# Split-precision hybrid layer and adaLN block: three attention rows in flight in layer two, value accumulators in two banks

## Chip, core and metric

One core of a Trainium2 chip runs the whole program, in one launch. The metric is the device time of one execution in microseconds (us); the lower the better. The kernel before takes 1076.02 us (median of 3 executions, 1075.15 to 1076.85).

## What is computed

All data are fp32: 512 tokens of width 1024. Layer one puts 16 meta tokens ahead of them and mixes a causal pooling branch with forgetting attention. Layer two is an adaLN block: eight stick-breaking heads and eight chunked heads with a relative-position bias, an output projection and a feed-forward part. Its heart:

```python
h = rmsnorm_2(x, g_norm1) * (1 + sc1) + sh1            # sc1, sh1, gt1, ... = silu(c) @ w_ada + b_ada
q_sb, k_sb, v_sb, q_ca, k_ca, v_ca = split(h @ w_in)   # 6 x 512 columns
# stick-breaking head, for each block of 128 queries
z = q_sb @ k_sb.T / 8
log_beta, log_1m = log_sigmoid(z), where(s < t, log_sigmoid(-z), 0)
w = where(s < t, exp(log_beta + suffix_sum(log_1m)), 0);  o_sb = w @ v_sb
# chunked head
q_ca, k_ca = rmsnorm_2(q_ca, g_q), rmsnorm_2(k_ca, g_k)
o_ca = softmax(q_ca @ k_ca.T / 8 + bias, masked to 9 chunks of 64) @ v_ca
x = x + gt1 * (concat(o_sb, o_ca) @ w_o)
h = rmsnorm_2(x, g_norm2) * (1 + sc2) + sh2
x = x + gt2 * (relu(h @ w1) ** 2 @ w2)
```

## The kernel before, in words

**Products.** A dense fp32 product is made of three matmuls (`mm3`, lines 149 to 152): every operand is split into a high part (a cast to fp32r, L131) and a low part (the rest, L128), and high x high, high x low and low x high are summed in one PSUM bank. Weights come through the staging buffers `wr` (four of them, 4 KB a partition), are cast by ACT (L131) and their low part is made by POOL or DVE (L128). A "dense triple" below is one such group of three.

**Order on PE.** Two generators run side by side in `weave`: `attn2()` issues the attention of layer two, `dense2()` the dense work around it. They share a planned clock, `clk[0]`, in nanoseconds of PE work. A generator that yields `at(t)` gets its turn again when the planned clock has reached t; till then the other one issues. The constants `LAT_*` (lines 37 to 44) are these allowances: how much planned PE time lies between a step and the step that needs its result. They order instructions only; the real waits are semaphores. What the other engines do, and in which order, is set by a scheduler out of the dependences and the program order, not by hand.

**Attention of layer two.** A unit is one row of scores: head pair p, head e of the pair, query block i (0 to 3, with 128(i+1) keys). 64 units, pairs in the order 0, 1, 4, 2, 5, 3, 6, 7; pairs 0 to 3 are stick-breaking (`stick`), 4 to 7 chunked (`soft`). A unit's scores are two matmuls (L438, L439) into a bank. For `stick`, ACT makes Abs, Exp, Ln (L947 to L949), DVE a maximum, a scan and a subtraction, ACT a last Exp (L953); for `soft`, DVE adds the bias and finds the maximum (L960), ACT makes the Exp (L962), DVE divides (L963, L964). The result x lies in a buffer of the tag "T" (five of 128x512). `turn` transposes x block by block on PE (L972), and ACT or DVE copies it into the head's tile `PT` (L975, L977). Two units later at the earliest (`LAG = 2`), and after the allowance `LAT_SB` or `LAT_CM`, a unit is turned. After the eight units of a pair, `pv2` multiplies them with the values (L908) and ACT copies the result (L911).

**Dense work beside it.** `DENSE` is the order of the pieces: q and k of the later pairs (`qk2_sb`, `qk2_ca`; 24 matmuls of 128x512 for one 128-column tile), and the values of columns 512 to 1023 in two pieces, `v2_chunk(2)` and `v2_chunk(3)`. The chunked heads' q and k are normed in `norm()`: ACT squares the tile, ACT and DVE split the squares (L131, L128, into `PTm`, two buffers), and PE sums them over each head with two matmuls (L870, L871), at `LAT_SQ` after the tile. `ada_step` puts the adaLN products in between (DVE L215, L217; PE L234). Then `wo_first` begins the output projection: its eight k take the normed attention results, and the weights of k = 4 to 7 are kept for the second half of the tokens in the tags "Y", "Y" (high and low of k = 4, 5), "Y" and "PT" (k = 6, 7).

**Value pieces.** `v2_chunk` (lines 801 to 813) makes 256 columns of values for four blocks of 128 tokens t. Weights come in two halves (kk = 0, 1); for each half, t runs over 0 to 3 with four dense triples of 128x256 each. Each t has a bank of its own. After the second half of a t, ACT copies its 256 columns out (L813).

**Opening.** x[0] is loaded, then the gain `norm_g`; four matmuls spread the gain over the partitions (L360), x[0] is squared by ACT (L323), normed (L329), transposed (L333), and the value products of layer one begin (L150 to L152).

Of the kernel before, what the change touches and what calls it, by code (L numbers as in the profile page):

```python
# [51 lines left out]
def hybrid_then_adaln_block(ctx, tc, a, out, tap=None):  # L52
    nc = tc.nc
# [80 lines left out]
    def weights(aps, shape, hi=None, lo=None, eng=None):  # L134
        raw = wts.tile([128] + shape, F32, name="wr", tag="wr", bufs=4)
# [13 lines left out]
    def mm3(ps, lh, ll, rh, rl, start, stop):  # L149
        pe.matmul(ps, lh, rh, start=start, stop=False)  # L150
        pe.matmul(ps, lh, rl, start=False, stop=False)  # L151
        pe.matmul(ps, ll, rh, start=False, stop=stop)  # L152
# [448 lines left out]
    def dense1():  # L601
# [199 lines left out]
    def v2_chunk(c):  # L801
        pss = [bank() for _ in range(4)]
        base = (1024, 1280, 2560, 2816)[c]
        for kk in range(2):
            wh, wl = weights([wcols(w_in2, 3 * D, base, 256, 4, 512 * kk)], [4, 256])
            for t in range(4):
                for q in range(4):
                    k = 4 * kk + q
# [173 lines left out]
    def attn2():  # L982
# [213 lines left out]
```

## Time and profile before

| | us |
|---|---|
| median of 3 executions | 1076.02 (1075.15 to 1076.85) |
| the profiled execution, its own time | 1077.35 |
| its span, first to last instruction | 1075.6 |
| PE busy | 1025.8 (95% of the span) |
| DVE busy | 538.7 (50%) |
| ACT busy | 532.5 (50%) |
| POOL busy | 306.4 (28%) |
| mean granted TensorE clock | 0.983 |

The shares are means over stages with different limits. In the trace the stages lie so: opening to 28 us, layer one to 400, the norms between the layers to 450, attention of layer two with its dense work from 450 to 690, the rest of the output projection and the feed-forward part to the end. A bracket at the end of a timeline row, as [1.93 <-DVE T L964], says how long the engine had been idle before it and which instruction's end released it.

### The profile page before, as it was taken

The numbers are of one execution on the slowest core, as the hardware profiler recorded it, in microseconds if no ns is written. First come the engines' busy times: TensorE is split into PE (matmuls) and PEld (weight loads), VectorE is DVE, ScalarE is ACT, GpSimd is POOL, SyncE is SP. The second block draws the span as 40 slices with busy tenths as digits, with TensorE's granted clock in tenths as the row PEclk, the third lists the DMA queues.
The fourth block names the chain that finished last, engine by engine and source line by source line (L and its number), as shares of the span: only waits on it lengthen the run. The fifth ranks groups of instructions, "written<-read, shape, count | busy, mean of one in ns | idle before, by whom it ended". The sixth has DMA issues, their size and how long they took to land.

```text
span 1075.6 us, 14076 instructions
## 1 busy us (share of the span) xinstructions
PE 1025.8 (95%) x5351; PEld 840.9 (78%) x5351; DVE 538.7 (50%) x1031; ACT 532.5 (50%) x1006; POOL 306.4 (28%) x146
## 2 busy tenths in 40 slices
PE   7999999999999998988799978999999999999998
PEld 6977987778888887977577756799888888888886
DVE  5365866873534588487867676672121002121115
ACT  6355654554454565476678776354334333222221
POOL 4222123423322541002112143112332233322330
PEclk9999999999999999999989989999999999999999
DMA  8332542454633656135332234433445322332212
GB/s 240 81 117 59 149 117 80 137 141 127 163 98 115 228 166 197 57 99 157 100 88 67 79 108 128 141 111 99 125 124 142 98 92 105 98 98 98 95 62 79
DMA packets 133973, 125.45 MB, mean 117 GB/s; under 512 B 6053, under 2 KB 110337, under 8 KB 133906
## 3 DMA queue, kind: packets, MB, share of 16 engines
q1 hardware_dynamic: 133906, 124.56, 38.7%
q8 instruction: 42, 0.69, 0.3%
q14 instruction: 25, 0.20, 0.1%
HBM read 119.82 MB, written 4.73 MB: 116 GB/s over the span
## 4 chain that ended last, share of the span: by engine, by line
PE 77%; DVE 11%; ACT 5%; DMA 3%; issue 2%; POOL 1%; SPq 0%; DVEq 0%; POOLq 0%; ACTq 0%
PE ps L150 23%; PE ps L151 22%; PE ps L152 22%; DMA wr<-in_w_in_dram 2%; DVE ada L217 2%; PE ps L972 2%; PE ps L908 2%; PE ps L519 1%; PE ps L438 1%; PE ps L439 1%; DMA wr<-in_w_ada_dram 1%; DVE T L951 1%; PE ps L234 1%; ACT wh L131 1%; DVE wl L128 1%
## 5 line engine op out<-in xcount | busy, mean ns | idle before, releaser
L128 POOL TENSOR_TENSOR wl<-wr,wh 128x1024 fp32r<-128x1024 f32 x105 | 258.1, 2460 | 672.6 <-ACT wh L131 666.3
L131 ACT CAST wh<-wr 128x1024 fp32r<-128x1024 f32 x142 | 148.6, 1048 | 304.4 <-PE ps L151 143.8
L150 PE MATMUL ps<-hh,wh 128*128 128x512 f32 (+1 forms) x352 | 130.1, 370 | 0.7 <-DVE nmx L483 0.7
L151 PE MATMUL ps<-hl,wh 128*128 128x512 f32 (+1 forms) x352 | 125.6, 357 | 0.0
L152 PE MATMUL ps<-hh,wl 128*128 128x512 f32 (+1 forms) x352 | 125.2, 356 | 0.0
L152 PE MATMUL ps<-wh,T 128*128 128x512 f32 x256 | 101.1, 395 | 0.0
L151 PE MATMUL ps<-wl,T 128*128 128x512 f32 x256 | 100.9, 394 | 0.0
L150 PE MATMUL ps<-wh,T 128*128 128x512 f32 x256 | 100.7, 393 | 0.0
L150 PE MATMUL ps<-QK,wh 128*128 128x512 f32 (+1 forms) x264 | 99.3, 376 | 0.0
L151 PE MATMUL ps<-PT,wh 128*128 128x512 f32 (+1 forms) x264 | 98.6, 373 | 0.0
L152 PE MATMUL ps<-QK,wl 128*128 128x512 f32 (+1 forms) x264 | 98.3, 373 | 0.0
L217 DVE SCALAR_TENSOR_TENSOR ada<-wr,vc,ada 128x512 f32<-128x512 f32 x84 | 78.0, 929 | 39.5 <-DMA wr<-in_w_ada_dram 38.6
L128 DVE TENSOR_TENSOR wl<-wr,wh 128x1024 fp32r<-128x1024 f32 x37 | 45.1, 1220 | 86.3 <-ACT wh L131 86.3
L150 PEld LDWEIGHTS ps<-hh,wh 128*128 128x128 f32 x352 | 66.6, 189 | 20.5 <-issue 10.8
L152 PEld LDWEIGHTS ps<-hh,wl 128*128 128x128 f32 x352 | 66.7, 189 | 9.8
L151 PEld LDWEIGHTS ps<-hl,wh 128*128 128x128 f32 x352 | 66.6, 189 | 7.8
L152 PEld LDWEIGHTS ps<-QK,wl 128*128 128x128 f32 x264 | 49.6, 188 | 9.8
L150 PEld LDWEIGHTS ps<-QK,wh 128*128 128x128 f32 x264 | 49.6, 188 | 9.7 <-ACT T L668 0.2
L151 PEld LDWEIGHTS ps<-wl,T 128*128 128x128 f32 x256 | 48.1, 188 | 11.5
L150 PEld LDWEIGHTS ps<-wh,T 128*128 128x128 f32 x256 | 48.2, 188 | 11.2
L152 PEld LDWEIGHTS ps<-wh,T 128*128 128x128 f32 x256 | 48.1, 188 | 11.3
L151 PEld LDWEIGHTS ps<-PT,wh 128*128 128x128 f32 x264 | 49.7, 188 | 9.1
(326 smaller groups left out, 2234.0 us busy)
## 6 DMA issues: line engine op xcount, KB each, us to landing
wr<-in_w_in_dram SPq DMA_DIRECT2D x64, 512.0 KB, 5.2
wr<-in_w_dram SPq DMA_DIRECT2D x64, 512.0 KB, 4.0
wr<-in_w_ada_dram SPq DMA_DIRECT2D x48, 512.0 KB, 3.8
wr<-in_w_out_dram SPq DMA_DIRECT2D x12, 512.0 KB
wr<-in_w_o_dram SPq DMA_DIRECT2D x12, 512.0 KB, 3.4
xr<-in_x_dram SPq DMA_DIRECT2D x8, 512.0 KB, 4.2
wr<-in_w_up_pool_dram SPq DMA_DIRECT2D x8, 256.0 KB, 2.6
wr<-in_w_up_attn_dram SPq DMA_DIRECT2D x8, 256.0 KB
```

The source lines that it names most:

```text
L128: (eng or pool).tensor_tensor(dst, raw, f(hi), op=OP.subtract)
L131: act.copy(dst_hi, raw)
L150: pe.matmul(ps, lh, rh, start=start, stop=False)
L151: pe.matmul(ps, lh, rl, start=False, stop=False)
L152: pe.matmul(ps, ll, rh, start=False, stop=stop)
L217: dve.scalar_tensor_tensor(acc, raw[:, q, :], cs, acc, op0=OP.mult, op1=OP.add)
L234: pe.matmul(ps[:, j:j + 1], acc[:, 128 * j:128 * j + 128], ones_f[:, :1], start=True, stop=True)
L438: pe.matmul(ps, A[e][:, sa], B[e][:, sb], start=True, stop=False)
L439: pe.matmul(ps, A[e][:, sa], L[e][:, sb], start=False, stop=stop)
L519: pe.matmul(po[64 * e:64 * e + 64, c0:], lhs, rhs, start=j < 0, stop=j == 3)
L908: pe.matmul(po[64 * e:64 * e + 64, 128 * j:], V2[j][:, hc], W[e][:, j, 128 * j:], start=j == 0, stop=j == 3)
L972: pe.transpose(pt[:, j, :], x[:, 128 * j:128 * j + 128], ident)
```

## The change

1. `attn2`: a unit is turned three units later at the earliest (`LAG` 3), and its allowance depends on the query block: `LAT_SB` (4000, 5500, 6500, 7500) and `LAT_CM` (3200, 3800, 4400, 5000) in place of 5200 and 3200. `LAT_CA`, `LAT_QK`, `LAT_SQ` and `LAT_PV` grow; `LAT_QK` and `LAT_PV` hold for layer one too.
2. A head's four rows x lie in one [128, 4, 512] tile of the tag "Y", which has four buffers and also holds `MX[1]` and the kept weights of the output projection; the buffers of "T" become 8, of "PTm" 4, of `wr` 5.
3. `v2_chunk` puts its four accumulators of 256 columns into two banks. Only the first matmul into a bank (k = 0 of an even t) carries the start flag.
4. The scratch space of the dynamic DMA descriptors is set to 1024 bytes a partition, which leaves room for 2.
5. Opening: `norm_g` is loaded ahead of x[0]; 6, 4 and 6 matmuls of a constant with itself (128x128 fp32) go to a bank that nobody reads: at the start, after the gain's matmuls, and after the first norm's transposes.

```diff
-LAT_CA = 5600.0
+LAT_CA = 6000.0
-LAT_SB = 5200.0
-LAT_CM = 3200.0
-LAT_QK = 2600.0
-LAT_SQ = 3800.0
+LAT_SB = (4000.0, 5500.0, 6500.0, 7500.0)
+LAT_CM = (3200.0, 3800.0, 4400.0, 5000.0)
+LAT_QK = 3800.0
+LAT_SQ = 5000.0
-LAT_PV = 600.0
+LAT_PV = 1500.0
...
-        raw = wts.tile([128] + shape, F32, name="wr", tag="wr", bufs=4)
+        raw = wts.tile([128] + shape, F32, name="wr", tag="wr", bufs=5)
...
-    BUFS = {"QK": 2, "PT": 3, "Y": 4, "V": 1, "T": 5, "Z": 2, "PTm": 2, "strip": 1, "Cm": 1, "Vm": 1}
+    BUFS = {"QK": 2, "PT": 3, "Y": 4, "V": 1, "T": 8, "Z": 2, "PTm": 4, "strip": 1, "Cm": 1, "Vm": 1}
...
+    sp.dma_start(gn, rows(a["norm_g"], 0, 1, D, 0, D))
     sp.dma_start(xr[0], rows(a["x"], 0, 128, D, 0, D))
-    sp.dma_start(gn, rows(a["norm_g"], 0, 1, D, 0, D))
+    idle = bank()
+    def warm(n):
+        for _ in range(n):
+            pe.matmul(idle[:, :128], ones_f, ones_f, start=True, stop=True)
+    warm(6)
...
         pe.matmul(gnb[b], ones_f[:1], gn[:, 512 * b:512 * b + 512], start=True, stop=True)
+    warm(4)
...
     first_norm(xr[0], 128, NM, *x0)
+    warm(6)
...
     def v2_chunk(c):
-        pss = [bank() for _ in range(4)]
+        pss = [b[:, 256 * q:256 * q + 256] for b in (bank(), bank()) for q in range(2)]
...
-                    mm3(pss[t][:, :256], h, l, wh[:, q, :], wl[:, q, :], k == 0, k == KT - 1)
+                    mm3(pss[t], h, l, wh[:, q, :], wl[:, q, :], k == 0 and t % 2 == 0, k == KT - 1,
+                        skip_group_check=True)
...
-                st[p, e] = wt([128, 4, 512], "PT")
+                st[p, e] = wt([128, 4, 512], "PT"), wt([128, 4, 512], "Y")
...
-            x = P[p, i, e] = wt([128, 512], "T")
+            x = st[p, e][1][:, i, :]
...
-        LAG = 2
+        LAG = 3
...
-                ripe[n] = clk[0] + (LAT_SB if p < 4 else LAT_CM)
+                ripe[n] = clk[0] + (LAT_SB if p < 4 else LAT_CM)[units[n][1]]
...
-    nc = bacc.Bacc("TRN2", target_bir_lowering=False, num_devices=1)
+    nc = bacc.Bacc("TRN2", target_bir_lowering=False, num_devices=1, dynamic_dma_scratch_size=1024)
```

Lines of the change stand 10 or 11 further on than those of the kernel before: L438 becomes L448, L972 becomes L982, L908 becomes L919, L813 becomes L824, L975 becomes L985.

Three places in the order of the instructions follow.

**PE, first head of pair 4.** From the scores of its fourth unit (L438, 128x512) to that unit's four transposes (L972 x4), before:

```order
L438 MATMUL ps<-QK 128x512
L439 MATMUL ps<-lz_590,QK 128x512
L972 MATMUL ps<-ident,T 128x128 x2
L438 MATMUL ps<-QK 128x256
L439 MATMUL ps<-lz_591,QK 128x256
L972 MATMUL ps<-ident,T 128x128 x3
L438 MATMUL ps<-QK 128x256
L439 MATMUL ps<-lz_591,QK 128x256
L150 MATMUL ps<-h2h,wh 128x512
L151 MATMUL ps<-h2l,wh 128x512
L152 MATMUL ps<-h2h,wl 128x512
L972 MATMUL ps<-ident,T 128x128 x4
```

and with the change, first the rows from those scores on (after them come the eight value products L919 of a pair),

```order
L448 MATMUL ps<-QK 128x512
L449 MATMUL ps<-lz_607,QK 128x512
L150 MATMUL ps<-h2h,wh 128x512
L151 MATMUL ps<-h2l,wh 128x512
L152 MATMUL ps<-h2h,wl 128x512
L150 MATMUL ps<-h2h,wh 128x512
L151 MATMUL ps<-h2l,wh 128x512
L152 MATMUL ps<-h2h,wl 128x512
L982 MATMUL ps<-ident,Y 128x128
```

and then the rows from behind the value products to the four transposes:

```order
L448 MATMUL ps<-QK 128x256
L449 MATMUL ps<-lz_608,QK 128x256
L234 MATMUL ps<-ones_f,ada 128x1 x4
L982 MATMUL ps<-ident,Y 128x128 x2
L448 MATMUL ps<-QK 128x256
L449 MATMUL ps<-lz_608,QK 128x256
L982 MATMUL ps<-ident,Y 128x128 x3
L448 MATMUL ps<-QK 128x384
L449 MATMUL ps<-lz_608,QK 128x384
L982 MATMUL ps<-ident,Y 128x128 x4
```

A further dense triple, the eight value products and the scores of a third unit now stand between a unit's scores and its transposes.

**PE, the first value piece, from t = 0 to t = 1 of the second half.** Before, each t has its own bank (ps_4504, ps_4505):

```order
L150 MATMUL ps_4504<-wh_4620,h2h_3374 128x256
L151 MATMUL ps_4504<-wl_4621,h2h_3374 128x256
L152 MATMUL ps_4504<-wh_4620,h2l_3376 128x256
L972 MATMUL ps_4636<-ident_78,T_4542 128x128 [waits Activation_49]
L150 MATMUL ps_4505<-wh_4620,h2h_3374 128x256
L151 MATMUL ps_4505<-wl_4621,h2h_3374 128x256
L152 MATMUL ps_4505<-wh_4620,h2l_3376 128x256
```

With the change t = 0 and t = 1 lie in ps_4515, and the first matmul of t = 1 waits for ACT:

```order
L150 MATMUL ps_4515<-wh_4638,h2h_3391 128x256
L151 MATMUL ps_4515<-wl_4639,h2h_3391 128x256
L152 MATMUL ps_4515<-wh_4638,h2l_3393 128x256
L150 MATMUL ps_4515<-wh_4638,h2h_3391 128x256 [waits Activation_49]
L151 MATMUL ps_4515<-wl_4639,h2h_3391 128x256
L152 MATMUL ps_4515<-wh_4638,h2l_3393 128x256
```

What it waits for is the copy of t = 0 (L824, V2<-ps_4515). This wait stands four times in the program, from t = 0 to 1 and from t = 2 to 3 in each of the two pieces.

**ACT, the end of the attention.** The casts of the kept weights of k = 6, 7 (L131, Y<-wr). Before, among the softmax rows of the last pair:

```order
L131 CAST mxs_6163<-Y_6101 128x512 [waits DMAHW6_49]
L131 CAST Y_6456<-wr_6458 128x1024 [waits DMAHW6_49]
L962 ACTIVATE T_6249,sums_6251<-T_6249,nmx_6250 128x128 [waits DVE_49]
L131 CAST Y_6456<-wr_6492 128x1024 [waits DMAHW7_49]
L962 ACTIVATE T_6264,sums_6266<-T_6264,nmx_6265 128x256 [waits DVE_49]
```

With the change, behind the copy of the last transposes of the attention (Y_6427 takes the buffer that these read):

```order
L985 COPY PT_6318<-ps_6394 128x2x128 [waits PE_49]
L131 CAST wh_6659<-wr_6657 128x1024 [waits DMAHW0_49]
L985 COPY PT_6318<-ps_6421 128x4x128 [waits PE_49]
L131 CAST Y_6427<-wr_6429 128x1024 [waits DMAHW4_49,DVE_49]
L131 CAST Y_6427<-wr_6457 128x1024 [waits DMAHW1_49]
```

The low part of the first (POOL, L128 PT<-wr,Y) follows it, and the matmuls of k = 6 stand on PE directly behind those transposes. In the same way the low part of k = 4, 5 takes the buffer of the head before, so that POOL waits for that head's last transposes (L982); on PE two score matmuls of 512 columns and one matmul of k = 4 stand between these and its use.

## Rows read from the trace of the kernel before

**Rows 1.** Stages: us; busy of PE, PEld, DVE, ACT, POOL (count); clock; DMA share; GB/s.

```profile
28.00:400.00 372.00, 367.16 (x1983) 300.22 (x1982) 221.83 (x427) 192.09 (x365) 121.11 (x54) 1.00 0.44 126
...
450.00:690.00 240.00, 211.47 (x1129) 165.32 (x1128) 171.42 (x372) 166.56 (x357) 49.38 (x20) 0.94 0.34 105
690.00:1075.00 385.00, 381.25 (x1786) 314.54 (x1784) 97.91 (x132) 130.99 (x191) 115.50 (x48) 1.00 0.33 101
```

**Rows 2.** Groups on PE, 440 to 700: busy, mean ns | idle before, releasers.

```profile
L972 PE MATMUL ps<-ident,T 128*128 128x128 f32 x160 | 31.7, 300 | 13.3 <-ACT T L953 4.7 <-DVE T L964 3.3 <-ACT Y L911 1.6
L438 PE MATMUL ps<-QK 128*128 128x256 f32 (+1 forms) x64 | 28.1, 439 | 2.5 <-ACT QK L433 2.5
L439 PE MATMUL ps<-lz,QK 128*128 128x256 f32 (+1 forms) x64 | 22.6, 354 | 3.6 <-DVE lz L434 3.6
...
L908 PE MATMUL ps<-PT,V 128*64 128x128 f32 (+3 forms) x128 | 19.7, 439 | 0.0
...
L871 PE MATMUL ps<-PTm,Cm 128*128 128x512 f32 x8 | 4.1, 509 | 5.5 <-DVE PTm L128 4.4 <-DVE Z L280 1.0
L870 PE MATMUL ps<-PTm,Cm 128*128 128x512 f32 x8 | 3.5, 444 | 2.3 <-ACT PTm L131 2.3
```

**Rows 3.** Timeline of PE: start, us, instruction, [idle before <-releaser].

```profile
453.44 0.39 PE L152 MATMUL ps<-h2h,wl 128*128 128x512 f32 x1
453.66 0.39 PE L150 MATMUL ps<-h2h,wh 128*128 128x512 f32 x1
...
494.39 1.11 PE L972 MATMUL ps<-ident,T 128*128 128x128 f32 x4 [2.76 <-ACT T L953]
...
534.05 0.66 PE L972 MATMUL ps<-ident,T 128*128 128x128 f32 x4 [1.93 <-DVE T L964]
```

**Rows 4.** Busy time in short stretches of the attention, columns as in Rows 1.

```profile
490.00:500.00 10.00, 6.97 (x31) 5.02 (x30) 8.51 (x16) 6.27 (x13) 0.00 (x0) 0.83 0.66 181
530.00:535.00 5.00, 3.07 (x20) 2.22 (x18) 4.91 (x13) 4.34 (x10) 1.09 (x1) 0.99 0.66 185
535.00:545.00 10.00, 8.60 (x31) 7.26 (x30) 5.80 (x21) 3.74 (x12) 1.27 (x1) 0.50 0.50 152
```

**Rows 5.** Timeline of PE and DVE in the opening.

```profile
4.34 3.75 PE L360 MATMUL ps<-QK,ones_f 1*128 1x512 f32 x4 [4.34 <-POOL lz L419]
...
12.49 0.42 PE L151 MATMUL ps<-Y,hh 128*128 128x256 f32 x1
...
14.67 2.04 DVE L161 SCALAR_TENSOR_TENSOR rs_r<-rs_t,rs_y 128x1 f32<-128x1 f32 x1
...
16.47 0.28 PE L150 MATMUL ps<-Y,hh 128*128 128x256 f32 x1
...
17.55 0.66 PE L333 MATMUL ps<-ident,PT 128*128 128x128 f32 x4 [0.56 <-DVE PT L329]
```

**Rows 6.** Timeline of PE between the layers.

```profile
409.02 0.39 PE L152 MATMUL ps<-Y,h2l 128*128 128x256 f32 x1 [1.98 <-DVE h2l L673]
...
425.01 0.33 PE L664 MATMUL ps<-ident,PTm 128*128 128x128 f32 x1 [3.00 <-DVE PTm L733]
```

**Rows 7.** PE and ACT: last matmul of a t, its copy; longest and shortest of eight.

```profile
489.96 0.28 PE L152 MATMUL ps<-wh,h2l 128*128 128x256 f32 x1
494.45 0.35 ACT L813 COPY V<-ps 128x256 f32<-128x256 f32 x1
...
600.43 0.28 PE L152 MATMUL ps<-wh,h2l 128*128 128x256 f32 x1
600.75 0.37 ACT L813 COPY V<-ps 128x256 f32<-128x256 f32 x1 [0.35 <-PE ps L152]
```

**Rows 8.** Kept weights of k = 6: cast on ACT, low part on POOL.

```profile
653.42 1.04 ACT L131 CAST Y<-wr 128x1024 fp32r<-128x1024 f32 x1
...
667.80 2.58 POOL L128 TENSOR_TENSOR PT<-wr,Y 128x1024 fp32r<-128x1024 f32 x1
```

**Rows 9.** Groups on ACT, whole span: the copy of four transposes.

```profile
L975 ACT COPY PT<-ps 128x512 f32<-128x512 f32 x16 | 9.2, 575 | 9.7 <-PE ps L972 9.7
```

More of the change, by code (lines that the diff above doesn't have):

```diff
@@ L147, in weights, with mm3 @@
         return hi, lo
[L149 to L152, printed above, removed]
+    def mm3(ps, lh, ll, rh, rl, start, stop, **go):
+        pe.matmul(ps, lh, rh, start=start, stop=False, **go)
+        pe.matmul(ps, lh, rl, start=False, stop=False, **go)
+        pe.matmul(ps, ll, rh, start=False, stop=stop, **go)
     def rstd(r, ss, n):
@@ L204, in ada @@
         half, k = j // 4, 2 * (j % 4)
-        raw = wts.tile([128, 2, 512], F32, name="wr", tag="wr", bufs=4)
+        raw = wts.tile([128, 2, 512], F32, name="wr", tag="wr", bufs=5)
         x = a["w_ada_2"]
@@ L607, in dense1 @@
                 ada_step(2)
-        raw = wts.tile([128, 4, 128], F32, name="wr", tag="wr", bufs=4)
+        raw = wts.tile([128, 4, 128], F32, name="wr", tag="wr", bufs=5)
         sp.dma_start(raw, bass.AP(tensor=a["pool_w"].tensor, offset=a["pool_w"].offset,
@@ L809, in v2_chunk @@
                     h, l = h_of(k, 128 * t, 128)
-                    mm3(pss[t][:, :256], h, l, wh[:, q, :], wl[:, q, :], k == 0, k == KT - 1)
+                    mm3(pss[t], h, l, wh[:, q, :], wl[:, q, :], k == 0 and t % 2 == 0, k == KT - 1,
+                        skip_group_check=True)
                     yield 325
                 if kk:
-                    act.copy(V2[t][:, 256 * c:256 * c + 256], pss[t][:, :256])
+                    act.copy(V2[t][:, 256 * c:256 * c + 256], pss[t])
     vw = [v2_weights(0), v2_weights(1)]
@@ L919, in hybrid_then_adaln_block @@
     away = []
-    st, Z, P = {}, {}, {}
+    st = {}
     strips = {}
@@ L967, in turn @@
         def turn(p, i, e):
-            x = P.pop((p, i, e))
-            PT = st[p, e]
+            PT, x = st[p, e][0], st[p, e][1][:, i, :]
             pt = bank().rearrange("p (j n) -> p j n", j=4)
@@ L1004, in attn2 @@
                 yield at(clk[0] + LAT_PV)
-                yield from pv2(p, [st[p, e] for e in range(2)])
+                yield from pv2(p, [st[p, e][0] for e in range(2)])
                 if p == LAST_SB:
```

## The prediction, made before the change was run

> **What bounds the kernel now.** I read the table of stages first, then the groups on PE, then the timeline round the longest idle times. The reader is to see that PE is the bound nearly everywhere: it is busy for 367.2 of 372 us in layer one and for 381.3 of 385 us after 690 [rows 1]. In the attention of layer two it works for only 211.5 of 240 us, at a mean granted clock of 0.94, while DVE has 171.4 and ACT 166.6 us to do [rows 1]. Two things can be won there: 28.5 us of idle PE, and about 0.06 x 240 = 14.4 us lost to the clock. The groups say where the idle time stands: 13.3 us ahead of the transposes (L972), 7.8 ahead of the sums of the norms (L870, L871), 6.1 ahead of scores (L438, L439), together 27.2 [rows 2]. The timeline says what such a wait is: four transposes wait 2.76 us for the last Exp of their row, others 1.93 us for DVE's division [rows 3]. The clock falls about the same places: in the ten microseconds after the wait at 534 the granted clock is 0.50, the 1.2 GHz level, with PE busy for 8.60 of them; round the wait at 494 it is 0.83 [rows 4].
>
> **Turns of the scores (LAG, LAT_SB, LAT_CM).** In the place shown, one dense triple more, the eight value products and a third unit's scores now stand between scores and transposes. A dense matmul of 512 columns takes 0.22 us, from start to start [rows 3], a triple so about 0.7; eight value products take 8 x 19.7 / 128 = 1.2 us, a transpose 31.7 / 160 = 0.2 us [rows 2]. With the scores that is some 2.5 us more; most other units get 1.5 to 2.5. That covers a wait of 1.93 and nearly one of 2.76. It doesn't take all of the 13.3, since a row that waits behind others on a busy engine comes later with them: DVE works for 4.91 of 5 us just ahead of the wait at 534 [rows 4]. I leave a third, 4.5 us: **-8.8** (ends -13.3 and -4).
>
> **Norms (LAT_SQ, PTm).** The allowance lets a whole tile of 24 matmuls pass in place of 18, so 6 x 0.22 = 1.3 us more for each of eight norms. Of 7.8 us I take away **-5.4** (ends -7.8 and -2).
>
> **First scores of a pair (LAT_CA).** 0.4 us more for each of four pairs: **-1.6** of 6.1 (ends -4 and 0).
>
> **Clock.** If about three fifths of the idle time goes, three fifths of the 14.4 go with it: **-9** (ends -14 and -2). It is the term that I can size least: one stretch at half clock alone costs 8.60 / 2 = 4.3 us [rows 4].
>
> **Value pieces in two banks: new waits.** Four times PE must now wait for ACT's copy of the other half of a bank, and there is nothing else on PE's list between. What this costs is the time from the last matmul of a t to the end of its copy. In the trace of before it is 489.96 + 0.28 = 490.24 to 494.80, or 4.56 us, at the longest, and 600.71 to 601.12, or 0.41 us, at the shortest [rows 7]; the eight sum to 9.6, 1.2 each. The ends are 4 x 0.41 = 1.6 and 4 x 4.56 = 18.2 us. The copy stands on ACT among the Abs, Exp and Ln of the rows of scores, one of which waits for DVE, so I take the mean: **+4.8**. If ACT runs empty while PE waits, the next scores come late, too; that is in the upper end.
>
> Before, a copy could end 4.56 us after its last matmul [rows 7] at no cost, since each accumulator had a bank of its own and no matmul waited for the copy. The Trainium skill ("PSUM — Partial Sum Buffer", section "PSUM bank collisions raise a hardware error") asks for semaphores by bank and quadrant, not by address; by it the new wait can't be argued away because the two halves have different columns, and it speaks against this part of the change. Were it by address, the term above would be 0 and the sum 4.8 lower.
>
> **Scores in "Y": the kept weights come late.** Before, the weights of k = 6 are cast at 653.42 and their low part is made at 667.80 [rows 8], both ahead of use. Now they need the buffer of the last head. Behind its last transposes come ACT's copy (0.58 [rows 9]), the cast (1.04) and POOL's low part (2.58 [rows 8]), while PE has one matmul (0.22) to do: 0.58 + 1.04 + 2.58 - 0.22 = 4.0 us. For k = 4, POOL's low part starts at the last transposes of the head before; PE has two score matmuls and one of k = 4 to do, about 0.7 us: 2.5 - 0.7 = 1.8 us. Together **+5.8**. The low end is 2 (casts and transposes overlap, POOL has an early start); the high end is 10, if POOL's four products ahead of it (4 x 2.5) are late.
>
> **Clock after the new waits.** Eight to ten microseconds of new idle in six places. The stretch round the wait of 2.76 lost 0.17 x 10 = 1.7 us [rows 4]; two of that size or a little less: **+3** (ends 0 and 9).
>
> **Rows with less allowance than before.** `LAT_SB` of the first query block falls from 5200 to 4000 ns. Eight stick-breaking heads by 1.2 us bound this by 9.6; since three units in flight set the distance in most cases, **+2** (ends 0 and 5).
>
> **Opening.** The value products take 0.42 us a matmul until 16 us and 0.28 after [rows 5], so an earlier fast start could save up to 1.9 us (half of 12.1 to 15.9). But the next transposes wait at 17.55 for DVE, 0.56 us even now [rows 5], and DVE's chain doesn't depend on PE: its L161 took 2.04 us there [rows 5]. The last six idle matmuls lie on the path: a quarter of a 512-column one, 3.75 / 4 / 4 = 0.23 each [rows 5], 1.4 us. I take **0** (ends -1.9, if DVE's 2.04 goes too, and +1.4). The other ten lie in idle time, 4.34 us ahead of the first matmul [rows 5].
>
> **Layer one** (LAT_QK, LAT_PV, PTm): 4.8 us of idle PE [rows 1], of which the longer allowance reaches few: **-1** (ends -3 and +1). **Between the layers** (fifth staging buffer): waits of 1.98 and 3.00 us [rows 6]; a load goes ahead sooner, but DVE's adaLN products then stand ahead of the parts PE waits for: **-1** (ends -4 and +2). After 690 PE has 3.8 us of idle time in 385 [rows 1]: nothing. The scratch size adds no instruction: nothing.
>
> **Sum:** -8.8 - 5.4 - 1.6 - 9 + 4.8 + 5.8 + 3 + 2 + 0 - 1 - 1 = -11.2. The profiled execution took 1077.35 us, so it would take 1066.1. It stood 1.3 us above the median of the three runs, 1076.02; against that the forecast is 1076.0 - 11.2, rounded to **1065 us**.
>
> **Rivals.**
> 1. *The new waits are covered.* PE comes to the shared bank when ACT has copied (four times 0.41 us, since ACT is busy for only 6.27 of 10 us near 494 [rows 4]), and the kept weights are ready or cost 2 us. Then 4.8, 5.8 and 3 become 1.6, 2 and 0: 1065 - 10 = 1055; with a little more of the waits gone, 1050. Against it: the orders shown have nothing between.
> 2. *The chain is bound by DVE, not by the allowance.* DVE is busy for 8.51 of 10 and 4.91 of 5 us about the waits [rows 4]. A longer allowance then only moves the wait: half of 15.8 and of 9 come back, 12.4 us: 1077, no change. In this case the longer allowances do nothing of what they say. Against it: over the stage DVE has 171 us in 240 [rows 1].
> 3. *Slower: the two banks.* If each of the four waits is like the longest row, 4.56 us, and brings the half clock, the price is 18.2 in place of 4.8 and 4 x 2.2 (half of a stretch as that after 534, 4.3 [rows 4]) beside it: 1065 + 13.4 + 8.8 = 1087. It decides from the point where a wait costs over 4.5 us with its clock. For it: the copy is put in ACT's order by the scheduler behind rows that wait for DVE, as at 490. Against it: seven of the eight copies of before took about 1 us or less.
>
> **How the numbers follow.** Forecast (1057 to 1071) 0.50; rival 1 (1049 to 1057) 0.17; rival 2 (1071 to 1080) 0.15; rival 3 (1080 to 1092) 0.15; anything else, mostly slower by something not seen here, 0.03. A measurement of this kernel can tell about 0.2%, 2.2 us, from no change. Below 1073.8 lie the forecast, rival 1 and a fifth to a quarter of rival 2: 0.71. Above 1078.2 lie rival 3, the rest and a little of rival 2: 0.20; between them 0.09. The range of 8 in 10 runs from 1051 to 1079: it holds the forecast, most of rivals 1 and 2, and leaves out rival 3.
>
> **What would show it.** Right: idle time ahead of L982 near 4.5 us and ahead of the norms' sums near 2.4, granted clock of the stage at 0.96 or more; four waits of about a microsecond ahead of L150 of 128x256 at a change of t; two waits for POOL, of some 2 and 4 us, ahead of L151 of the output projection. Wrong: idle time ahead of L982 still near 13 (rival 2), waits of 4 us or more in the value pieces (rival 3), none at all at either place (rival 1), or a change of more than 4 us outside 450 to 690.

## The result, and the profile after

The change takes 1065.56 us (median of 4 executions, 1064.52 to 1066.70), against 1076.43 of the kernel before in the same comparison: a ratio of 0.9897, 95% interval 0.9877 to 0.9917, or 11 us faster. The forecast was 1065.

The page, part 1, after: PE is busy for 2.5 us less than before, in a span that is 12.8 us shorter (1062.8).

```profile
PE 1023.3 (96%) x5383; PEld 841.9 (79%) x5383; DVE 528.4 (50%) x1031; ACT 533.3 (50%) x1006; POOL 306.3 (29%) x146
```

The stages after, columns as in [rows 1]:

```profile
28.00:400.00 372.00, 369.39 (x2008) 303.32 (x2007) 215.06 (x433) 197.15 (x376) 121.93 (x56) 1.00 0.45 129
...
450.00:690.00 240.00, 216.08 (x1175) 170.28 (x1174) 174.65 (x375) 164.77 (x352) 55.13 (x23) 0.96 0.36 110
```

The idle share of the attention has shrunk by 4.6 us and its clock rose from 0.94 to 0.96 [rows 1]. Since the work now slides through this window, stages are better compared by the start of the same matmul in both timelines of PE (one profiled execution of each kernel):

| matmul | before | after | the stretch up to it changed by |
|---|---|---|---|
| first dense one of 512 columns (L150 hh,wh) | 47.13 | 48.37 | +1.2 |
| first of layer two (L150 Y,h2h) | 405.21 | 401.68 | -4.8 |
| first scores of layer two (L438, now L448) | 448.32 | 443.31 | -1.5 |
| last of the output projection | 709.77 | 695.34 | -9.4 |
| last of all | 1070.86 | 1058.01 | +1.6 |

The groups on PE after, 440 to 690 (they answer to [rows 2]; L982 was L972, L448 and L449 were L438 and L439, L881 and L882 were L870 and L871):

```profile
L982 PE MATMUL ps<-ident,Y 128*128 128x128 f32 x160 | 30.2, 292 | 5.1 <-DVE nmx L971 2.2 <-DVE Y L975 2.1 <-DVE QK L437 0.8
L448 PE MATMUL ps<-QK 128*128 128x256 f32 (+1 forms) x64 | 27.2, 425 | 0.0
L449 PE MATMUL ps<-lz,QK 128*128 128x256 f32 (+1 forms) x64 | 22.3, 348 | 3.1 <-DVE lz L444 3.1
L919 PE MATMUL ps<-PT,V 128*64 128x512 f32 (+3 forms) x128 | 20.4, 444 | 1.0 <-DVE PT L987 1.0
L150 PE MATMUL ps<-wh,h2h 128*128 128x256 f32 x64 | 19.3, 302 | 1.7 <-ACT V L824 1.7
...
L150 PE MATMUL ps<-Y,mxs 128*128 128x512 f32 x32 | 13.5, 422 | 3.0 <-ACT Y L131 1.6 <-ACT mxs L131 1.3
...
L151 PE MATMUL ps<-PT,mxs 128*128 128x512 f32 x16 | 6.9, 431 | 1.9 <-POOL PT L128 1.9
L151 PE MATMUL ps<-Y,mxs 128*128 128x512 f32 x16 | 6.5, 409 | 2.6 <-POOL Y L128 2.6
L234 PE MATMUL ps<-ones_f,ada 128*128 128x1 f32 x32 | 4.8, 272 | 3.8 <-DVE ada L217 3.8
L881 PE MATMUL ps<-PTm,Cm 128*128 128x512 f32 x8 | 3.5, 440 | 0.1
L882 PE MATMUL ps<-PTm,Cm 128*128 128x512 f32 x8 | 3.4, 419 | 0.5 <-DVE PTm L128 0.5
```

The old waits have shrunk: 13.3 us ahead of the transposes are now 5.1, 7.8 ahead of the norms 0.6, 6.1 ahead of the scores 3.1. New ones stand beside them: 1.7 at the value pieces, 6.1 at the kept weights (ACT 1.6, POOL 1.9 and 2.6), 3.8 at the adaLN products (L234), 1.0 at the values (L919). The timeline of PE after has them one by one:

```profile
475.30 0.39 PE L150 MATMUL ps<-wh,h2h 128*128 128x256 f32 x1 [0.46 <-ACT V L824]
...
526.37 1.86 PE L234 MATMUL ps<-ones_f,ada 128*128 128x1 f32 x8 [3.81 <-DVE ada L217]
...
648.78 0.50 PE L151 MATMUL ps<-Y,mxs 128*128 128x512 f32 x1 [1.94 <-POOL Y L128]
...
658.10 0.50 PE L150 MATMUL ps<-Y,mxs 128*128 128x512 f32 x1 [1.62 <-ACT Y L131]
660.53 0.50 PE L151 MATMUL ps<-PT,mxs 128*128 128x512 f32 x1 [1.93 <-POOL PT L128]
```

The last two are the chain that was forecast from the order: the copy of the last transposes, the cast, POOL's low part. In the timelines of ACT and POOL it reads:

```profile
656.52 0.59 ACT L985 COPY PT<-ps 128x512 f32<-128x512 f32 x1 [3.22 <-PE ps L982]
657.00 2.00 ACT L131 CAST Y<-wr 128x1024 fp32r<-128x1024 f32 x2
...
658.13 2.35 POOL L128 TENSOR_TENSOR PT<-wr,Y 128x1024 fp32r<-128x1024 f32 x1 [0.62 <-ACT Y L131]
```

### The profile page after: what moved, and what is told of

It is laid out like the page before. It is cut to its first block, busy times and chain, and to the rows that moved or that the text cites. A ratio compares the mean times of both kernels' runs of the same rounds, so it can differ in the third digit from the quotient of the medians.

```text
span 1062.8 us, 14132 instructions
## 1 busy us (share of the span) xinstructions
PE 1023.3 (96%) x5383; PEld 841.9 (79%) x5383; DVE 528.4 (50%) x1031; ACT 533.3 (50%) x1006; POOL 306.3 (29%) x146
## 4 chain that ended last, share of the span: by engine, by line
PE 76%; DVE 10%; ACT 5%; issue 4%; POOL 2%; DMA 2%; SPq 1%; DVEq 0%; POOLq 0%; ACTq 0%
PE ps L150 23%; PE ps L151 22%; PE ps L152 22%; DVE ada L217 2%; PE ps L919 1%; PE ps L529 1%; PE ps L982 1%; DVE Y L962 1%; PE ps L448 1%; DMA wr<-in_w_ada_dram 1%; PE ps L449 1%; ACT wh L131 1%; POOL Y L128 1%; PE ps L234 1%; POOL wl L128 1%
## 5 line engine op out<-in xcount | busy, mean ns | idle before, releaser
L128 POOL TENSOR_TENSOR wl<-wr,wh 128x1024 fp32r<-128x1024 f32 x105 | 257.8, 2458 | 668.4 <-ACT wh L131 662.4
L131 ACT CAST wh<-wr 128x1024 fp32r<-128x1024 f32 x142 | 148.9, 1050 | 179.7 <-PE ps L151 145.8
L150 PE MATMUL ps<-hh,wh 128*128 128x512 f32 (+1 forms) x352 | 129.1, 367 | 0.2 <-DVE nmx L493 0.2
L152 PE MATMUL ps<-hh,wl 128*128 128x512 f32 (+1 forms) x352 | 124.5, 354 | 0.0
L128 DVE TENSOR_TENSOR wl<-wr,wh 128x1024 fp32r<-128x1024 f32 x37 | 46.6, 1261 | 115.9 <-ACT wh L131 115.9
L150 PE MATMUL ps<-QK,wh 128*128 128x512 f32 (+1 forms) x264 | 99.3, 376 | 1.9 <-ACT T L678 1.9
L150 PE MATMUL ps<-wh,T 128*128 128x512 f32 x256 | 101.1, 395 | 0.0
L152 PE MATMUL ps<-wh,T 128*128 128x512 f32 x256 | 100.6, 393 | 0.0
L152 PE MATMUL ps<-QK,wl 128*128 128x512 f32 (+1 forms) x264 | 98.4, 373 | 0.0
L217 DVE SCALAR_TENSOR_TENSOR ada<-wr,vc,ada 128x512 f32<-128x512 f32 x84 | 73.9, 880 | 18.3 <-DMA wr<-in_w_ada_dram 17.4
L150 PEld LDWEIGHTS ps<-hh,wh 128*128 128x128 f32 x352 | 66.2, 188 | 16.8 <-issue 7.5
L152 PEld LDWEIGHTS ps<-hh,wl 128*128 128x128 f32 x352 | 66.2, 188 | 9.7
L150 PEld LDWEIGHTS ps<-QK,wh 128*128 128x128 f32 x264 | 49.6, 188 | 11.7 <-ACT T L678 2.1
L152 PEld LDWEIGHTS ps<-QK,wl 128*128 128x128 f32 x264 | 49.6, 188 | 9.8
L152 PEld LDWEIGHTS ps<-wh,T 128*128 128x128 f32 x256 | 48.1, 188 | 11.6
L150 PEld LDWEIGHTS ps<-wh,T 128*128 128x128 f32 x256 | 48.1, 188 | 11.1
L151 PEld LDWEIGHTS ps<-wl,T 128*128 128x128 f32 x256 | 48.1, 188 | 10.9
```

Of the source, the lines that this page charges most:

```text
L128: (eng or pool).tensor_tensor(dst, raw, f(hi), op=OP.subtract)
L131: act.copy(dst_hi, raw)
L150: pe.matmul(ps, lh, rh, start=start, stop=False, **go)
L151: pe.matmul(ps, lh, rl, start=False, stop=False, **go)
L152: pe.matmul(ps, ll, rh, start=False, stop=stop, **go)
L217: dve.scalar_tensor_tensor(acc, raw[:, q, :], cs, acc, op0=OP.mult, op1=OP.add)
```

## The experiments

The kernel before had medians between 1073.4 and 1076.4 us in the several comparisons, so kernels of different comparisons are held against each other by their ratio to it; 0.001 is about 1.1 us. The intervals are some 0.002 to 0.003 to each side. Waits, clocks and stretches come from the one profiled execution of each kernel. All experiments start from the change, unless another is named.

**x of the scores in T again** (`e3_x_in_T`):

```diff
-                st[p, e] = wt([128, 4, 512], "PT"), wt([128, 4, 512], "Y")
+                st[p, e] = wt([128, 4, 512], "PT")
...
-            x = st[p, e][1][:, i, :]
+            x = P[p, i, e] = wt([128, 512], "T")
...
```

> The change with the rows x of the scores in buffers of the tag T again (eight of them), so that the kept weights of the output projection find free buffers of Y. Theory A: the waits for POOL and ACT ahead of the matmuls of k = 4 to 7 (1.94, 0.70, 1.62 and 1.93 us, 6.2 together) go, and with them some clock: 1058.5 to 1060 us. Theory B: something else is late there next (the last rows' softmax or the split of the mixed heads), and only a part comes back: 1062 to 1065.

Measured: 1058.74 us, 0.9842 (0.9818 to 0.9867), 0.0055 or some 6 us better than the change. The groups on PE, 440 to 690, keep the transposes' short wait, and of the kept weights' waits nothing is left; the 1.3 at the split of the mixed heads was there before as well:

```profile
L983 PE MATMUL ps<-ident,T 128*128 128x128 f32 x160 | 30.0, 291 | 3.9 <-DVE T L975 3.1 <-DVE QK L437 0.7
...
L150 PE MATMUL ps<-Y,mxs 128*128 128x512 f32 x32 | 12.9, 402 | 1.3 <-ACT mxs L131 1.3
```

Theory A. Lending the buffers of Y to the scores cost the change these 6 us, net: ahead of the scores PE waits 5.9 us here in place of 3.1. Eight buffers of T do for three units in flight.

**Two units in flight** (`e4_T_lag2`, from e3; with x in Y it wasn't tried) **and three with flat allowances** (`e10_T_lag3_flat`, from e3):

```diff
-        LAG = 3
+        LAG = 2
...
-LAT_SB = (4000.0, 5500.0, 6500.0, 7500.0)
-LAT_CM = (3200.0, 3800.0, 4400.0, 5000.0)
+LAT_SB = (5200.0,) * 4
+LAT_CM = (3200.0,) * 4
```

(the second without the first two lines)

> As e3_x_in_T, but with two units in flight and the turn allowances of before (5200 and 3200). Theory A: the longer way from scores to transposes is what the change won in the attention: idle time ahead of the transposes back to about 13 us and the clock of the stage to 0.94, so 10 to 15 us above e3_x_in_T, near 1072. Theory B: the buffers (eight T, four PTm, five staging) did it: within 3 us of e3_x_in_T.

> As e3_x_in_T, with three units in flight but the flat turn allowances of before (5200 and 3200). Theory A: the third unit sets the distance from scores to transposes in most places, the tables add little: 1058 to 1061 us, under 7 us of waits ahead of the transposes. Theory B: the tables do it: near e4_T_lag2, 1064 to 1067, with 10 us or more of waits there.

Measured: 0.9924 (0.9901 to 0.9947) and 0.9915 (0.9897 to 0.9934), against 0.9842 of e3. With two units the transposes wait as before, and the clock of 440 to 680 is 0.94:

```profile
L983 PE MATMUL ps<-ident,T 128*128 128x128 f32 x160 | 30.9, 293 | 13.2 <-ACT T L964 6.9 <-DVE sums L974 3.7 <-DVE T L975 2.2
```

With three units and flat allowances the same groups read:

```profile
L983 PE MATMUL ps<-ident,T 128*128 128x128 f32 x160 | 30.2, 291 | 2.3 <-DVE T L975 2.1
...
L150 PE MATMUL ps<-wh,h2h 128*128 128x256 f32 x64 | 20.2, 315 | 6.3 <-ACT V L824 6.3
```

The first is theory A in its mechanism. The price, 9 us (7.5 by the medians, which come from one comparison), is a little under its range; 9.3 us more at the transposes and the lower clock stand against the 3.8 us at L234, which aren't there with two units. The second splits the theories: the waits ahead of the transposes are as A says (the third unit alone takes them to 2.3), the time as B says. What is missing against e3 stands elsewhere: 6.3 us in place of 1.7 at the shared value banks, 3.0 in place of 0.6 at the norms, and a clock of 0.95 in place of 0.96 from 440 to 680. One of the waits at the value banks, in the timelines of ACT and PE:

```profile
481.91 0.61 ACT L957 ACTIVATE T<-ps 128x512 f32<-128x512 f32 x1
...
482.59 0.65 ACT L958 ACTIVATE T<-T 128x512 f32<-128x512 f32 x1
483.11 0.39 ACT L824 COPY V<-ps 128x256 f32<-128x256 f32 x1
...
483.55 0.39 PE L150 MATMUL ps<-wh,h2h 128*128 128x256 f32 x1 [2.44 <-ACT V L824]
```

The copy stands on ACT behind the rows of stick-breaking heads, and PE waits for these, too. The term that the prediction took from the mean of eight copies is thus real, and 1.7 or 6.3 by where the order puts the pieces.

**The norms' allowances** (`e5_T_norms`, from e3). On the change itself, with x in Y, the same edit (`e5_norms`) ends in a deadlock; which instructions would wait for each other stays open.

```diff
-LAT_SQ = 5000.0
-LAT_CA = 6000.0
+LAT_SQ = 3800.0
+LAT_CA = 5600.0
```

> As e3_x_in_T, with the allowances of the norms and of the pairs' first scores as before (LAT_SQ 3800, LAT_CA 5600). Theory A: the longer allowance is what took the waits ahead of the sums of the norms away (7.8 us before, 0.6 in e3_x_in_T): they come back to 4 us or more and the time is 1062 to 1065 us. Theory B: the four PTm buffers did it: within 2 us of 1058.7, and under 1.5 us of waits there.

Measured: 1064.64 us, 0.9921 (0.9903 to 0.9940), and the waits are back, 9.4 us:

```profile
L882 PE MATMUL ps<-PTm,Cm 128*128 128x512 f32 x8 | 3.9, 488 | 5.9 <-DVE PTm L128 5.9
L881 PE MATMUL ps<-PTm,Cm 128*128 128x512 f32 x8 | 3.8, 470 | 3.5 <-ACT PTm L131 3.4
```

Theory A: four PTm buffers with the old allowance leave the norms 9.4 us of waits, against 7.8 before. In the same run the wait ahead of the transposes fell from 3.9 to 0.8, so a part of what was lost only moved. Ahead of the scores PE waits 3.1 us with the old LAT_CA, so no gain of LAT_CA is seen there.

**No allowance at all, buffers and banks only** (`e7_T_all_old_lat`): the edits of e4, of e5 and of e6 below together,

```diff
-LAT_CA = 6000.0
-LAT_QK = 3800.0
-LAT_SQ = 5000.0
-LAT_PV = 1500.0
+LAT_CA = 5600.0
+LAT_QK = 2600.0
+LAT_SQ = 3800.0
+LAT_PV = 600.0
```

> Only the buffers and banks, no allowance: x in T, two units in flight and all allowances as before, with eight T, four PTm, five staging buffers, two value banks and the idle products. Theory A: the buffers win layer one's wait at 66 us and part of the norms, 3 to 6 us below before, near 1071; the allowances win the rest. Theory B: the buffers are worth nothing without the allowances: 1075 or more. Theory C: the buffers are worth most of the change: 1066 or less.

Measured: 1073.82 us, 1.0006 (0.9992 to 1.0020). By the time measured it is theory B: the buffers, the two banks and the idle products together are worth nothing measurable. But that is a sum of gains and losses, as the trace shows. Layer one is faster, as theory A has it: the wait at 66 us is gone, and from the first dense matmul to the first of layer two it takes 354.20 us (before 358.08, the change 353.31). Against that the opening takes 1.2 us more and the shared value banks bring new waits (groups on PE, 440 to 690):

```profile
L150 PE MATMUL ps<-wh,h2h 128*128 128x256 f32 x64 | 20.0, 313 | 5.0 <-ACT V L824 5.0
```

From the first scores of layer two to the last of the projection it takes 259.20 us (before 261.45, the change 252.03): there most of the gain comes with the allowances. The two profiled executions differ by 3.5 us, the medians by nothing; executions of the kernel before spread over 5 us in this comparison. So the ratio falls in steps from 1.0006 (no allowance) to 0.9924 (allowances of norms and scores, LAT_QK, LAT_PV: e4), to 0.9842 (third unit and its tables: e3), and the scores in Y take 0.0055 back.

**Layer one** (`e6_qk`, `e9_wr4`):

```diff
-LAT_QK = 3800.0
-LAT_PV = 1500.0
+LAT_QK = 2600.0
+LAT_PV = 600.0
```

and, in the other,

```diff
-        raw = wts.tile([128] + shape, F32, name="wr", tag="wr", bufs=5)
+        raw = wts.tile([128] + shape, F32, name="wr", tag="wr", bufs=4)
```

(and the same number in two more places).

> The change with LAT_QK 2600 and LAT_PV 600. In layer one the change won 4.7 us, 3.5 of them between 61 and 78 us, where a wait of 1.74 us (L481 on DVE's Cm) and a clock of 0.79 over 8 us stood before. Theory A: it is LAT_QK, which puts a dense triple more ahead of L481: the wait comes back with the low clock, about 1069 us. Theory B: the fifth staging buffer or the other buffers did it: 1065 to 1066, no wait there.

> The change with four staging buffers. Theory A: the fifth made the wait at the second norm between the layers 1.41 us in place of 3.00 and nothing else: 1067 us, with the wait back at about 3. Theory B: it also covers casts in the attention, so 1069 or more. Theory C: nothing changes, 1065.6.

Measured: 1060.39 us, 0.9875 (0.9848 to 0.9901) and 1063.00 us, 0.9895 (0.9869 to 0.9921), neither to be told from the change with certainty. The loss that theory A expected of e6 and theory B of e9 isn't there; the 1.4 us of e9's theory A are too few to be seen. The traces tell more. Before, PE waited at L481 (now L491; timeline of PE), and from 68 to 72 us the granted clock was 0.67, between the two levels of 1.2 and 2.4 GHz (busy time in a short stretch, columns as in [rows 1]):

```profile
66.15 0.38 PE L481 MATMUL ps<-Cm,sel 128*128 128x256 f32 x1 [1.74 <-DVE Cm L653]
```

```profile
68.00:72.00 4.00, 4.00 (x16) 3.19 (x15) 1.07 (x6) 1.71 (x4) 0.17 (x1) 0.67 0.04 15
```

With e6 there is no wait and the clock stays up (first fence, its stretch from 68 to 72); with e9 a wait of 0.66 is left (second fence, PE), and the clock of that stretch is 1.00, too:

```profile
68.00:72.00 4.00, 4.00 (x24) 3.36 (x23) 2.45 (x9) 3.59 (x9) 2.41 (x1) 1.00 0.00 0
```

```profile
66.98 0.38 PE L491 MATMUL ps<-Cm,sel 128*128 128x256 f32 x1 [0.66 <-DVE Cm L663]
...
422.61 0.33 PE L674 MATMUL ps<-ident,PTm 128*128 128x128 f32 x1 [3.03 <-DVE PTm L743]
```

In e7, with the old LAT_QK and five buffers, there is no wait either. So either the fifth staging buffer or the longer LAT_QK takes most of this wait; each was tried with the larger T and PTm, whose part stays open. The second row of e9 is the wait between the layers: with four staging buffers it is 3.03, as before [rows 6], with five 1.41 in the change. But with five it is 2.75 in e1, e6, e7 and e11 and 2.74 in e8, and 1.41 to 1.51 in the other runs. So most of the step from 3.0 to 1.4 isn't shown to be the buffer's; what makes it stays open. On e6's attention, faster than the change's, see below.

**Opening** (`e1_no_idle`):

```diff
-    sp.dma_start(gn, rows(a["norm_g"], 0, 1, D, 0, D))
     sp.dma_start(xr[0], rows(a["x"], 0, 128, D, 0, D))
+    sp.dma_start(gn, rows(a["norm_g"], 0, 1, D, 0, D))
...
-    warm(6)
...
-    warm(4)
...
-    warm(6)
```

> The change without the idle products, and with x[0] loaded first again. In the trace of the change the end of the opening (the value products near 29 us) stands 1.2 us later than before. Theory A: the last six idle products only stand in the way and the late start of x[0] does the rest; taking them out gives those 1.2 us back: about 1064.3 us. Theory B: they hold the clock up and pay for themselves; without them the value products take 0.41 us again until 16 us and the time is 1065.6 or more. If the wait for POOL's low part at 19.13 us (1.52 us) stays without them, it comes from another part of the change.

Measured: 1062.83 us, 0.9890 (0.9865 to 0.9916); the ratio can't tell 1 us. PE's timeline, the change first:

```profile
13.53 0.36 PE L150 MATMUL ps<-Y,hh 128*128 128x256 f32 x1
13.74 0.28 PE L151 MATMUL ps<-Y,hh 128*128 128x256 f32 x1
...
19.13 0.39 PE L151 MATMUL ps<-Y,hh 128*128 128x264 f32 x1 [1.52 <-POOL Y L128]
```

and without the idle products:

```profile
12.22 0.56 PE L150 MATMUL ps<-Y,hh 128*128 128x256 f32 x1
12.57 0.41 PE L151 MATMUL ps<-Y,hh 128*128 128x256 f32 x1
```

With the idle products the first value products run at 0.28 in place of 0.41 us. But they begin 1.3 us later, and what is won by 17 us is waited for at 19 (POOL's low part). The first dense matmul of 512 columns starts at 47.25 without them and at 48.37 with them: theory A, by 1.1 us in the trace. The other traces agree but for one: with the idle products it starts between 48.33 and 48.37 in eight kernels, without them between 46.97 and 47.47 in five, the kernel before among them; in e2, whose opening is the change's, it starts at 46.78. There the four matmuls of the gain took 2.12 us in place of 3.78, and why in this execution only stays open. The wait at 19.13 went with the idle products or with the order of the two loads; the two weren't parted.

**Four value banks** (`e2_four_banks`):

```diff
-        pss = [b[:, 256 * q:256 * q + 256] for b in (bank(), bank()) for q in range(2)]
+        pss = [bank()[:, :256] for _ in range(4)]
...
-                    mm3(pss[t], h, l, wh[:, q, :], wl[:, q, :], k == 0 and t % 2 == 0, k == KT - 1,
-                        skip_group_check=True)
+                    mm3(pss[t], h, l, wh[:, q, :], wl[:, q, :], k == 0, k == KT - 1)
```

> The change with four banks for a value piece, as before. Theory A: the shared banks cost just the waits that the trace shows ahead of L150 at a change of t, 0.46, 0.58 and 0.65 us: about 1063.9 us, and no idle time ahead of L150 of 128x256. Theory B: beside the wait itself they cost the clock and late scores behind it: 1060 to 1062. Theory C: the banks that the pieces now hold keep others waiting: 1066 or more.

Measured: 1064.69 us, 0.9905 (0.9876 to 0.9934): no gain over the change's 0.9897. The three waits at the value pieces are gone, as theory A says, and some 6 us behind the first piece PE waits for a weight's low part on DVE (groups on PE, 440 to 690, and timeline):

```profile
L152 PE MATMUL ps<-h2h,wl 128*128 128x512 f32 x112 | 44.6, 399 | 4.0 <-DVE wl L128 4.0
```

```profile
492.77 0.79 PE L152 MATMUL ps<-h2h,wl 128*128 128x512 f32 x1 [4.01 <-DVE wl L128]
```

That was 1.0 with the change. Theory B's gain of some 4 us or more isn't there; theory A's 1.7 us are too few for the ratio, but the stretch from the first scores to the last of the projection takes 253.78 us, 1.75 more than with the change. The wait moved on, and it grew: the low part itself took 3.21 us in place of 1.2 (see the last section).

**A version that beats both** (`e8_best`: the edits of e1 and e3 and the first pair of lines here), **the same with the second pair** (`e11_best_pv`) **or with the edit of e2** (`e12_best_banks`):

```diff
-LAT_ADA = 4000.0
+LAT_ADA = 8000.0
...
-LAT_PV = 1500.0
+LAT_PV = 600.0
```

> Three things at once, for a version that beats both: no idle products, x of the scores in T, and LAT_ADA 8000 in place of 4000, as L234 waits 3.81 us for DVE's L217 at 526 us with the change. Theory A: the three add up: e3_x_in_T at 1058.7, less 1.2 to 2.7 for the opening, less 4 to 5 for the adaLN wait and its clock: 1051 to 1054 us. Theory B: the wait at 526 only moves to the scores or transposes behind it: 1056 to 1057.

> As e8_best with LAT_PV 600 in place of 1500. In e6_qk (LAT_QK 2600, LAT_PV 600) the attention of layer two ran 6 us faster than with the change, at a clock of 0.99. Theory A: that is LAT_PV, the value products of a pair come sooner and the pieces behind them meet fewer waits: 1048 to 1052 us. Theory B: it came from where the waits happened to fall in that order, not from LAT_PV: within 2.5 us of 1054.5, on either side.

> As e8_best with four banks for the value pieces. In e8_best the shared banks cost waits of 3.34, 1.29 and 0.64 us ahead of L150 of 128x256. Theory A: without them 4 to 6 us less with their clock: a ratio to the kernel before of 0.976 to 0.978 (e8_best 0.9815). Theory B: as in e2_four_banks, the wait moves to the next thing on PE's list (DVE's low part of a weight, L152, or the scores): a ratio of 0.979 to 0.982. Theory C: the four banks keep others waiting and it is slower than e8_best.

Measured: e8 1054.49 us, 0.9815 (0.9790 to 0.9840); e11 0.9862 (0.9842 to 0.9882); e12 1054.13 us, 0.9805 (0.9784 to 0.9825). e8 is below the change by 0.0082, some 9 us; the wait at L234 is gone and the clock of 440 to 680 is 0.98. Its median lies just above theory A's range; by the ratios it is 2.9 us below e3, where theory A says 5 to 8 and theory B about 2. The stretch from the first scores to the last of the projection is 5.5 us shorter than e3's, though the value pieces wait 5.3 us in place of 1.7. So the wait moved in part, and the two theories aren't parted. e11 is slower than e8 by 0.0047, outside both theories: a shorter LAT_PV is no gain here. So it isn't LAT_PV by itself that made e6's attention fast; the shorter LAT_QK, which e6 has too, wasn't tried on e8. In e12 theory B holds once more: its gain over e8, 0.0010, is within the intervals. The groups of e8 and of e12, and the low part that PE waits for in e12 (timelines of POOL and DVE):

```profile
L150 PE MATMUL ps<-wh,h2h 128*128 128x256 f32 x64 | 19.7, 308 | 5.3 <-ACT V L815 5.3
```

```profile
L872 PE MATMUL ps<-PTm,Cm 128*128 128x512 f32 x8 | 3.5, 443 | 4.7 <-DVE PTm L128 4.7
```

```profile
495.30 5.10 POOL L128 TENSOR_TENSOR wl<-wr,wh 128x1024 fp32r<-128x1024 f32 x2 [3.32 <-ACT wh L131]
...
498.13 2.82 DVE L128 TENSOR_TENSOR PTm<-T,PTm 128x512 fp32r<-128x512 f32 x1
```

The 5.3 us go, and 4.7 come at the first norm, at 501 us; the two longer waits of e8 ended at 477 and 488. As in e2 the low part that PE waits for is a long one: 2.82 us, where the same operation takes 0.7 in the change's trace when POOL is free.

## Why the prediction was right

The forecast of 1065 rested on a sum, and eight of its eleven terms come within about 2 us of the traces:

| term | predicted | in the traces |
|---|---|---|
| turns of the scores | -8.8 | -8.2 (13.3 to 5.1) |
| norms | -5.4 | -7.2 (7.8 to 0.6) |
| first scores of a pair | -1.6 | -3.0 (6.1 to 3.1) |
| clock, lost and newly lost | -9 + 3 = -6 | -4.8 (0.06 to 0.04 of 240 us) |
| value pieces | +4.8 | +1.7 |
| kept weights | +5.8 | +6.2 (1.94, 0.70, 1.62, 1.93) |
| rows with less allowance | +2 | not found as such |
| waits without a term (L234, L919, L152) | none | +5.8 |
| opening | 0 | +1.2 |
| layer one | -1 | -4.8 |
| between the layers | -1 | -1.5 |
| after 690 | 0 | +1.6 |

**Right, and shown by experiment.** In the attention the allowances win the time, not the buffers alone: without the allowances 2.3 of the 9.4 us are won there (e7), with two units the 13 us come back (e4), with the old LAT_SQ the norms' waits (e5). Whether the allowances would win as much with the old numbers of buffers wasn't run. The kept weights cost what the chain copy, cast and low part adds up to, and putting x back in T returns it (e3). Rival 2, a bound by DVE, is refuted: DVE has 175 us of 240 to do, 171 before, and the waits went. The clock term is right to about 2 us at best, as it comes from figures with two decimals.

**Size near, cause open: the first scores.** The 3.0 us at the first scores were put down to LAT_CA. With the old LAT_CA PE waits 3.1 us there (e5), with the old LAT_QK 4.5 (e6); the first scores of the stick-breaking pairs go by LAT_QK, which the sum counts for layer one alone. What won the 3.0 stays open.

**Mis-sized: the value pieces.** The wait is there, three times of four, at 0.46, 0.58 and 0.65 us, nearer to the shortest copy [rows 7] than to the mean. That is rival 1's 1.6 us; its other half, kept weights that are ready, didn't come. The Trainium skill's rule ("PSUM — Partial Sum Buffer", section "PSUM bank collisions raise a hardware error") asks for such waits by bank; the rows of L150 released by L824 agree that PE waits here though its columns are others. What would happen without the wait no run shows. But the size isn't a property of the kernel: it was 1.7, 5.3 and 6.3 us in three orders of the same pieces, and where the banks were parted PE waited 3.0 us more (e2) and 4.7 us (e12) elsewhere. Rival 3's 18 us were never seen.

**Failed: the cover of layer one.** The step "4.8 us of idle PE, of which the longer allowance reaches few: -1" counted idle time alone. The wait of 1.74 at 66 us also brought the clock of 0.67 just behind it. The same matmuls start 1.2 us later than before at 53 us and 2.3 earlier at 78, so the place was worth 3.5; the mean clock of the stage, 1.00 in [rows 1], hid it. A change of over 4 us outside the attention was named as a sign of being wrong, and this is one. The step also put the fifth staging buffer down to the time between the layers only, while either that buffer or LAT_QK suffices to end most of this wait (e6, e7, e9). The term between the layers, -1, came to -1.5, but it isn't shown to be the buffer's (2.75 us in five runs that have it).

**Failed: what is late next.** The sum had no term for the wait at L234 (3.81), nor for the 1.0 each at L919 and L152. In the order of the change PE reaches the adaLN sums while DVE still alternates between their terms (L217) and the softmax; with two units in flight the wait isn't there (e4). The only loss that the sum left room for beside the new waits, +2 for rows with less allowance, falls short of these 5.8 by 3.8 us. Layer one's error of the other sign, -3.8, the value pieces, -3.1, and the larger gains at norms and scores made up for it and for the opening and the end. So the total is better than its parts, and that it came within 1 us of the forecast is luck. The terms measured sum to -13 in the two profiled executions, whose spans differ by 12.8; the medians differ by 10.9, since the profiled execution before lies 0.9 us above its median, and the one after 1.0 below.

**Opening and end.** The upper end of the opening's range was +1.4; it came to +1.2, since the six idle products lie on the path and the faster products behind them run into POOL. The six took 2.2 us (11.37 to 13.53), not the 1.4 of the sum. After 690 a new wait of 1.89 us stands at 710.76, for ACT's scaling in the second norm, behind a DVE that waits 3.64 us for a load of adaLN weights: "nothing" was wrong there, as it looked at idle time of before alone.

## To carry to other kernels

A longer allowance between a product and its use is worth what it takes from the waits, clock included, minus what becomes late next; here the gross gain in the attention was some 23 us and the net 9 (single executions). Before a buffer is lent to another use, look up who takes it next in the order: the six microseconds at the end stand there in three lines. And when undoing a cost brings nothing (four banks, twice), look at the same stretch of the timeline for the wait that took its place, before calling the cost unreal.

## What was not expected of the hardware

A DVE instruction with its tensors in SBUF that falls beside a POOL tensor operation can take several times its length. With the change the scan of 512 columns at 493.64 (timelines of POOL and DVE):

```profile
493.29 2.67 POOL L128 TENSOR_TENSOR wl<-wr,wh 128x1024 fp32r<-128x1024 f32 x1 [1.86 <-ACT wh L131]
...
493.64 3.41 DVE L962 TENSOR_TENSOR_SCAN Y<-ones_f,Y 128x512 f32<-128x512 f32 x1
```

with four value banks, where POOL is free by then:

```profile
489.29 2.35 POOL L128 TENSOR_TENSOR wl<-wr,wh 128x1024 fp32r<-128x1024 f32 x1 [0.86 <-ACT wh L131]
...
489.51 3.21 DVE L128 TENSOR_TENSOR wl<-wr,wh 128x1024 fp32r<-128x1024 f32 x1
492.64 1.21 DVE L961 TENSOR_TENSOR_SCAN Y<-ones_f,Y 128x512 f32<-128x512 f32 x1
```

The scan takes 1.21 us alone and 3.41 beside POOL: it ends 1.1 us after POOL's end, a little under its own length. DVE's low part, 1.2 us elsewhere, takes 3.21 in the same way, and it is the one that PE waits for in e2. Both cases and their opposite stand together in the trace of the change (timelines of POOL and DVE):

```profile
555.82 3.12 POOL L128 TENSOR_TENSOR wl<-wr,wh 128x1024 fp32r<-128x1024 f32 x1 [15.55 <-ACT wh L131]
```

```profile
555.53 1.22 DVE L962 TENSOR_TENSOR_SCAN Y<-ones_f,Y 128x512 f32<-128x512 f32 x1
556.78 0.69 DVE L963 TENSOR_TENSOR Y<-ps,Y 128x512 f32<-128x512 f32 x1
557.39 2.65 DVE L128 TENSOR_TENSOR wl<-wr,wh 128x1024 fp32r<-128x1024 f32 x1
```

This scan began ahead of POOL and kept its 1.22 us, and POOL's operation took 3.12 in place of 2.4. The next one, L963, reads one operand from PSUM and kept its 0.69 us beside POOL. The low part, with both in SBUF, began behind POOL and took 2.65. Of the 32 operations `xs<-ps,xs` of 128x512 in this trace half begin beside such a POOL operation, and all take 0.68 or 0.69 us. Two tensors in SBUF aren't the only case: DVE's division L975 of 128x512, with one, took 1.79 us at 641.39 beside POOL and 0.48 or 0.49 elsewhere. The Trainium skill ("SBUF — State Buffer", section "SBUF: two separate sides") says that of a DVE operation with two SBUF inputs and a GpSimd one that reads SBUF the one that starts first holds a shared pair of ports for its whole instruction, while the other is blocked; these rows agree. The 2.04 us of DVE's L161 in [rows 5] lie beside such a POOL operation, too. Some of the waits for DVE, those of e2 and e12 above, are so in part waits for POOL; a kernel without POOL's low parts there wasn't run.
